# The last ConvFFN's up-products as seven half products per channel chunk instead of eight, its down-products in six groups

## The chip, the core and the metric

The kernel runs on one core of a Trainium2 chip. The metric is the device time of one execution in microseconds. TensorE (PE) does the matrix products, VectorE (DVE), ScalarE (ACT) and GpSimd (POOL) the element work, SyncE (SP) issues the weight transfers.

## What is computed

The model is one inference step of four layers on 128 context tokens and 512 latent tokens, 640 columns in all, with a model width of 1024. Each layer is a token mixer and then a gated ConvFFN, both on a normed and modulated input. The last layer's FFN is what the change touches:

```python
def _conv_ffn(h, w_up, conv_w, conv_b, w_down):
    g, u = jnp.split(h @ w_up, 2, axis=-1)       # h: tokens x 1024, w_up: 1024 x 5632
    g = _dwconv3(g, conv_w) + conv_b              # three taps along the tokens
    return (jax.nn.gelu(g, approximate=False) * u) @ w_down   # 2816 x 1024

# in _layer, for every layer:
    h = _modulate(_rmsnorm(x, P["norm2_w"][li]), sh2, sc2)
    x = x + g2[:, None, :] * _conv_ffn(h, ...)
```

## The kernel before

Activations lie with channels on the 128 partitions and tokens along the row. There are 642 columns: two that carry the modulation's shift terms, 128 of context, 512 of latents. The width 1024 is eight chunks of 128 channels (`KC`), the FFN's 2816 hidden channels are 22 chunks (`NF`), numbered f.

Every fp32 operand of a product is held as a rounded part and a remainder (names ending in h and l, XH and XL for the FFN's input). A product is three matmuls on these, h by h, h by l and l by h, for each chunk of the contraction (`mm3`). An up-product of one channel chunk is 8 chunks x 3 x 2 PSUM banks (322 and 320 columns) = 48 matmuls.

The program is a list of units, each with one weight block and a function (`unit`). The weight pipeline runs two blocks ahead (`prefetch`): SP fetches a block to `wraw` (three buffers), ACT casts it to `wh`, and DVE subtracts to get `wl` (three buffers each). Inside an engine instructions run in the order of its queue. A scheduler set that order when the kernel was built.

In the FFN, chunk f has two units, gate and up. DVE multiplies each result out of PSUM by the per-token norm `rB` (`evac`, L400). The gate then goes to `gp` on ACT (`with_bias`, L404/405), through the three taps on ACT and twice DVE (`conv3`, L420 to L422) and through Gelu on ACT (L464). DVE multiplies gate and up into `hd` (L467/468), and ACT and DVE split that into `hh` and `hl` (L410/411). After 8, 15 and 22 chunks (`THIRDS`) come eight units down, one for each output chunk d, with 8 or 7 hidden chunks as contraction. DVE adds each result to x (`x_update`, L371/372). The very last product is cut in two (`tail`), and the final norm follows.

PSUM has three two-bank buffers (`mm`) and two one-bank buffers (`smp`) in the last layers. The work pool holds three buffers of `ev`, three of `gc` and two of `hd`.

Of the kernel before, what the change touches and what calls it, by code (L numbers as in the profile page):

```python
# [77 lines left out]
def build(tc, a, plan=None):  # L78
# [96 lines left out]
    def mod(l, v, k):  # L175
        return mods[l][:, _ada_pos(v, k)]
# [17 lines left out]
    def wload(src):  # L194
        return wsplit(*wfetch(src))

    def unit(src, fn, barrier=False):
        stream["units"].append((src, fn, barrier))

    def prefetch(upto):  # L200

        us = stream["units"]
        while stream["seen"] < min(upto, stream["cap"]):
            i = stream["load"]
            if i >= len(us) or (us[i][2] and i > stream["at"]):
# [20 lines left out]
    def chunks(t, n, m=P):  # L226
        return t[:, : n * m].rearrange("p (k m) -> p k m", m=m)
# [154 lines left out]

    wk = dict(stack=None, pool=None)

    def open_work():
# [27 lines left out]

    def conv3(gp, cols, bias):

        gc = wk["pool"].tile([P, 676], F32, tag="gc", bufs=3, name="gc")[:, 0 : T + 1]
# [12 lines left out]

    def ffn(l, nxt):  # L430
        ctx = ExitStack()
        cell = dict(o={}, hid=[])

        def start():
            cell["pool"] = ctx.enter_context(tc.tile_pool(name="hid", bufs=9, reuse_waits="tile"))
# [35 lines left out]
            return fn  # L471

        def down(i, d):
            f0, f1 = THIRDS[i]

            def fn(wh, wl):
                hid = cell["hid"][f0:f1]
                hs, ls = [h for h, _ in hid], [lo for _, lo in hid]
                if nxt is None and i == 2 and d == KC - 1:
# [6 lines left out]
                x_update(d, o, mod(l, G2, d), final=(nxt,) if i == 2 else None)  # L486

            return fn


        for f in range(NF):
            unit(a["ffn_up"][l, f], up(f, 0))
            unit(a["ffn_up"][l, NF + f], up(f, 1))
            for i, (_, f1) in enumerate(THIRDS):
                if f == min(f1, NF - 1):
                    for d in range(KC):
                        unit(a[f"ffn_dn{i}"][l, d], down(i, d))
        unit(None, ctx.close)

    def tail(l, d, products):  # L500
# [831 lines left out]
    def fourier(nxt):  # L1332
# [163 lines left out]
        def place():  # L1496
            for g in range(NFG):
                for s_, d_ in zip(c["ny"], (c["fH"], c["fL"])):
                    G.dma_start(d_[2 * g + 1][0:1].bitcast(F32), s_[g : g + 1].bitcast(F32))
            fl.close()  # L1500
            open_ada(boot, 2, True)
            open_xa("left")

        def out(d):
            def fn(wh, wl):
# [294 lines left out]
```

## Time and profile before

| | before |
|---|---|
| median of 3 runs | 2715.08 us (2712.8 to 2715.26) |
| profiled execution | 2714.8 us, of which 2713.0 us are the span of the profile |
| PE busy | 2659.0 us, 98% of the span |
| DVE, ACT, POOL busy | 1803.0, 1030.0 and 119.2 us |
| the chain that ended last | PE 94%, DVE 3%, ACT 1% |

Busy shares are means over the whole program. What bounds a stage is read from a window of that stage and from what its engines waited for: behind an instruction's row in brackets stands the idle time before it and what ended it.

### The profile page before, as it was taken

Reading aid. Unit: us, or ns where it says so; the run is one execution under the profiler, and the core shown is the slowest. Engines: PE = TensorE matmul, PEld = TensorE weight load, DVE = VectorE, ACT = ScalarE, POOL = GpSimd, SP = SyncE. Lnnn points to the kernel's source line nnn. Section 1 sums busy time; section 2 is a strip of 40 time slices with the busy share of each in tenths; the row PEclk is TensorE's granted clock in tenths of the full one; section 3 lists DMA queues with packets and bytes.
Section 4 is the critical chain, followed back from the end, with each engine's and each line's share of the span. In section 5 each row is a group of like instructions: output and inputs, shape, how many; then the busy total and the mean of one; then the engine's idle time right before and its main releaser. Section 6 shows DMA issues by size and latency. Waiting matters only on the chain.

```text
span 2713.0 us, 43697 instructions
## 1 busy us (share of the span) xinstructions
PE 2659.0 (98%) x18071; PEld 2597.5 (96%) x18071; DVE 1803.0 (66%) x2855; ACT 1030.0 (38%) x1593; POOL 119.2 (4%) x153
## 2 busy tenths in 40 slices
PE   7999999999999999999999999999999999999998
PEld 6788888999999999999999999999999999999998
DVE  4677887999935689994455599954555555535354
ACT  4565675332323443232345332332332233323231
POOL 0222220000000000000001000000000000000000
PEclk9999999999999999999999999999999999999999
DMA  6223121566422325652223256622222222222221
GB/s 233 88 95 107 30 68 56 172 193 199 152 78 71 110 94 179 201 163 72 81 68 99 88 186 195 194 78 78 71 78 74 75 74 76 71 78 72 76 74 60
DMA packets 87814, 291.97 MB, mean 108 GB/s; under 512 B 11120, under 2 KB 16928, under 8 KB 87104
## 3 DMA queue, kind: packets, MB, share of 16 engines
q1 hardware_dynamic: 83808, 282.72, 33.1%
q0 software_dynamic: 2368, 4.92, 0.6%
q8 instruction: 143, 2.34, 0.4%
q10 hardware_dynamic: 1440, 1.53, 0.2%
q14 instruction: 55, 0.45, 0.1%
HBM read 283.72 MB, written 2.77 MB: 106 GB/s over the span
## 4 chain that ended last, share of the span: by engine, by line
PE 94%; DVE 3%; ACT 1%; issue 1%; DMA 1%; POOL 0%; POOLq 0%; DVEq 0%; SPq 0%; ACTq 0%
PE mm L242 80%; PE smp L763 3%; PE mm L878 1%; PE smp L900 1%; PE adaacc L166 1%; PE smp L916 1%; PE smp L915 1%; PE mm L877 1%; PE smp L809 1%; DMA adaraw<-in_ada_w 1%; PE mm L1436 1%; PE smp L337 0%; PE mm L643 0%; PE mm L1390 0%; PE mm L644 0%
## 5 line engine op out<-in xcount | busy, mean ns | idle before, releaser
L242 PE MATMUL mm<-XH,wh 128*128 128x320 f32 (+2 forms) x3248 | 750.0, 312 | 3.1 <-ACT sq L296 1.7
L242 PE MATMUL mm<-XH,wl 128*128 128x320 f32 (+2 forms) x3248 | 746.8, 311 | 0.0
L242 PE MATMUL mm<-XL,wh 128*128 128x320 f32 (+2 forms) x3248 | 745.3, 311 | 0.3 <-DVE XL L321 0.3
L190 ACT CAST wh<-wraw 128x1024 fp32r<-128x1024 f32 (+3 forms) x353 | 349.5, 991 | 961.9 <-PE mm L242 856.6
L242 PEld LDWEIGHTS mm<-XH,wh 128*128 128x128 f32 (+1 forms) x3248 | 547.3, 189 | 3.8 <-ACT sq L296 1.9
L242 PEld LDWEIGHTS mm<-XL,wh 128*128 128x128 f32 (+1 forms) x3248 | 548.1, 189 | 0.6 <-DVE XL L321 0.6
L242 PEld LDWEIGHTS mm<-XH,wl 128*128 128x128 f32 (+1 forms) x3248 | 548.0, 189 | 0.0
L191 DVE TENSOR_TENSOR wl<-wraw,wh 128x1024 fp32r<-128x1024 f32 (+3 forms) x333 | 394.7, 1185 | 28.7 <-ACT wh L190 27.6
L158 DVE CUSTOM_DVE_ANT_0 adajunk<-adaraw,adarow,sm 128x1024 f32<-128x1024 f32 x304 | 389.0, 1280 | 4.6 <-DMA adaraw<-in_ada_w 1.6
L400 DVE TENSOR_TENSOR ev<-mm,rB 128x642 f32<-128x642 f32 x200 | 164.9, 825 | 305.5 <-PE mm L242 299.9
L242 PE MATMUL mm<-hh,wh 128*128 128x320 f32 (+1 forms) x1536 | 350.5, 309 | 0.0
L242 PE MATMUL mm<-hh,wl 128*128 128x320 f32 (+1 forms) x1536 | 350.4, 309 | 0.0
L242 PE MATMUL mm<-hl,wh 128*128 128x320 f32 (+1 forms) x1536 | 350.1, 309 | 0.0
L242 PEld LDWEIGHTS mm<-hl,wh 128*128 128x128 f32 x1536 | 256.8, 188 | 0.0
L242 PEld LDWEIGHTS mm<-hh,wh 128*128 128x128 f32 x1536 | 256.8, 188 | 0.0
L242 PEld LDWEIGHTS mm<-hh,wl 128*128 128x128 f32 x1536 | 256.6, 188 | 0.0
L371 DVE SCALAR_TENSOR_TENSOR x<-mm,mod,x 128x128 f32<-128x128 f32 x111 | 38.9, 350 | 293.5 <-PE mm L242 293.4
L410 ACT CAST hh<-hd 128x640 fp32r<-128x640 f32 x96 | 69.9, 728 | 208.6 <-DVE hd L468 190.8
L464 ACT ACTIVATE gc<-gc 128x641 f32<-128x641 f32 x88 | 65.4, 743 | 176.4 <-DVE gc L422 176.3
L421 DVE SCALAR_TENSOR_TENSOR gc<-gp,conv,gc 128x641 f32<-128x641 f32 x88 | 77.9, 886 | 53.8 <-ACT gc L420 53.8
L411 DVE TENSOR_TENSOR hl<-hd,hh 128x640 fp32r<-128x640 f32 x96 | 79.0, 823 | 45.7 <-ACT hh L410 45.7
L420 ACT ACTIVATE gc<-gp,conv 128x641 f32<-128x641 f32 x88 | 81.5, 926 | 2.9
(333 smaller groups left out, 2994.4 us busy)
## 6 DMA issues: line engine op xcount, KB each, us to landing
adaraw<-in_ada_w SPq DMA_DIRECT2D x192, 512.0 KB, 3.8
wraw<-in_ffn_up SPq DMA_DIRECT2D x176, 512.0 KB, 3.6
wraw<-in_ffn_dn SPq DMA_DIRECT2D x64, 448.0 KB, 3.2
wraw<-in_ffn_dn SPq DMA_DIRECT2D x32, 512.0 KB, 3.7
wraw<-in_sconv_win SPq DMA_DIRECT2D x24, 512.0 KB, 3.6
wraw<-in_wo SPq DMA_DIRECT2D x8, 512.0 KB, 3.6
wraw<-in_fnet_w SPq DMA_DIRECT2D x8, 512.0 KB, 3.6
wraw<-in_sconv_wout SPq DMA_DIRECT2D x8, 512.0 KB, 3.5
```

The lines of the kernel that those rows point to most:

```text
L158: V.tensor_tensor_reduce(junk, w, ada["row"][:, r], 1.0, vec("adab", l * 48 + h * 8 + k), ALU.mult, ALU.add, m)
L190: S.copy(h[:, :n], raw[:, :n])
L191: (eng or V).tensor_tensor(lo[:, :n], raw[:, :n], h[:, :n].bitcast(F32), ALU.subtract)
L242: TE.matmul(o[:m, c0:c1], w_[:, k], x_[k][:, x0 : x0 + c1 - c0], start=st, stop=sp)
L371: V.scalar_tensor_tensor(x[:, d, 0:TP], o[:, lo : lo + TP], g[:, 0:1], x[:, d, 0:TP], ALU.mult, ALU.add)
L400: V.tensor_tensor(t[:m], o[:m, 190:832], st["rB"][:m], ALU.mult)
L410: S.copy(h, v)
L411: V.tensor_tensor(lo, v, h.bitcast(F32), ALU.subtract)
L420: S.activation(gc, gp[:, 1:642], AF.Identity, bias=bias, scale=cols[:, 1:2])
L421: V.scalar_tensor_tensor(gc, gp[:, 0:641], cols[:, 0:1], gc, ALU.mult, ALU.add)
L464: S.activation(gc, gc, AF.Gelu)
L763: TE.matmul(o[:, 0 : c1 - c0], w_[:, k], x_[k][:, c0:c1], start=st_, stop=sp)
```

## The change

In the last layer (`seven`), chunks 0 to 2 stay as they are. For f = 3 to 21 the two 1024 x 128 weight blocks (gate and up) and the 642 columns of the input are cut into halves. That makes a 2 x 2 by 2 x 2 block product: two halves of the contraction (four chunks each), gate and up, left 322 and right 322 columns (they overlap by two). Instead of eight products of half size the kernel does seven, on sums and differences of the blocks (Winograd's form of Strassen's scheme):

- `operands(k)`, four times: POOL adds XH and XL back together for two chunks (128 x 642), DVE forms four differences of 322 columns, ACT casts them, and DVE splits them. k = 0, 1 stand behind chunk 1 and k = 2, 3 behind chunk 2.
- `weights(f, j)`, j = 0 to 3: both blocks of f are fetched at j = 0. POOL makes three combinations at j = 0 and one at j = 2, each 128 x 512. ACT and DVE cast and split seven half blocks.
- `up7(f, j)`: seven `product`s of 12 matmuls of 322 columns, each in a one-bank `smp` buffer. ACT copies the first result to `m1`, DVE adds the others out of PSUM into `tg` and `tu` (seven additions) and then multiplies both by `rB`. `gated` and `later` put the bias, conv, Gelu and `hd` of chunk f between the products of chunk f+1. For chunk 21 they follow at once.
- The down-products come in six groups (`SMALL`), after chunks 4, 8, 12, 15, 18 and 21, of 4, 4, 4, 3, 3 and 4 hidden chunks: 48 units of half the length instead of 24.
- Ahead of the last layer's mixer `drop` opens the pools anew: two buffers of `ev` and `gc` instead of three, PSUM with two `mm` and four `smp` buffers instead of three and two.

```diff
...
+SMALL = ((0, 4, 0, 0), (4, 8, 0, 4), (8, 12, 1, 0), (12, 15, 1, 4), (15, 18, 2, 0), (18, 22, 2, 3))
+HW = 322
+NORMAL = 3
+SUMS = ((), (0, 1), (2, 3))
...
+        LEFT, RIGHT = slice(0, HW), slice(W - HW, W)
+
+        def operands(k):
...
+                for d in (k, k + 4):
+                    t = wk["pool"].tile([P, W], F32, tag="ev", bufs=wk["bufs"], name="ev")
+                    G.tensor_tensor(t, st["xh"][d].bitcast(F32), st["xl"][d].bitcast(F32), ALU.add)
+                    b.append(t)
+                (b11, b12), (b21, b22) = [(t[:, LEFT], t[:, RIGHT]) for t in b]
+                u = [wk["pool"].tile([P, 676], F32, tag="hd", name="hd") for _ in range(2)]
+                t1, t2, t3, t4 = [u[i // 2][:, i % 2 * HW : i % 2 * HW + HW] for i in range(4)]
+                V.tensor_tensor(t1, b12, b11, ALU.subtract)
+                V.tensor_tensor(t2, b22, t1, ALU.subtract)
+                V.tensor_tensor(t3, b22, b12, ALU.subtract)
+                V.tensor_tensor(t4, b21, t2, ALU.subtract)
+                for t, (h, lo) in zip((t1, t2, t3, t4), cell["t"]):
+                    S.copy(h[:, k], t)
+                    V.tensor_tensor(lo[:, k], t, h[:, k].bitcast(F32), ALU.subtract)
...
+        def weights(f, j):
...
+                def part(i, v):
+                    c_ = slice(i * 512, i * 512 + 512)
+                    S.copy(h[:, c_], v)
+                    V.tensor_tensor(lo[:, c_], v, h[:, c_].bitcast(F32), ALU.subtract)
+
+                if j == 0:
+                    s3 = cell["s3"] = cell["pool"].tile([P, 512], F32, tag="s3", bufs=1, name="s3")
+                    part(0, a11)
+                    G.tensor_tensor(s3, a11, a21, ALU.subtract)
+                    G.tensor_tensor(a21, a21, a22, ALU.add)
+                    G.tensor_tensor(a11, a21, a11, ALU.subtract)
+                    part(1, a11)
+                elif j == 1:
+                    part(0, cell["s3"])
+                    part(1, a22)
+                elif j == 2:
+                    part(0, a21)
+                    part(1, a12)
+                    G.tensor_tensor(a12, a12, a11, ALU.subtract)
+                else:
+                    part(0, a12)
...
+        def product(o, i, wh, wl, xh, xl):
...
+            for k in range(4):
+                for w_, x_, e in ((h, xh, False), (h, xl, False), (lo, xh, k == 3)):
+                    TE.matmul(o[:, 0:HW], w_[:, k], x_[k], start=k == 0 and x_ is xh and w_ is h, stop=e)
...
+                if j == 0:
+                    product(o, 0, wh, wl, *half(0, LEFT))
+                    product(q, 1, wh, wl, *sums(1))
+                    S.copy(m1, o[:, 0:HW])
+                    V.tensor_tensor(tg[:, RIGHT], m1, q[:, 0:HW], ALU.add)
+                    later()
+                elif j == 1:
+                    product(o, 0, wh, wl, *sums(2))
+                    product(q, 1, wh, wl, *sums(3))
+                    V.tensor_tensor(tu[:, RIGHT], tg[:, RIGHT], o[:, 0:HW], ALU.add)
+                    V.tensor_tensor(tu[:, 0:n], tu[:, n : 2 * n], q[:, 0:n], ALU.add)
+                    later()
+                elif j == 2:
+                    product(o, 0, wh, wl, *sums(0))
+                    product(q, 1, wh, wl, *half(4, LEFT))
+                    V.tensor_tensor(tu[:, RIGHT], tu[:, RIGHT], o[:, 0:HW], ALU.add)
+                    V.tensor_tensor(tg[:, RIGHT], tg[:, RIGHT], o[:, 0:HW], ALU.add)
+                    V.tensor_tensor(tu, tu, rB, ALU.mult)
+                    V.tensor_tensor(tg[:, 0:n], m1[:, 0:n], q[:, 0:n], ALU.add)
+                else:
+                    product(o, 0, wh, wl, *half(4, RIGHT))
+                    V.tensor_tensor(tg[:, RIGHT], tg[:, RIGHT], o[:, 0:HW], ALU.add)
+                    V.tensor_tensor(tg, tg, rB, ALU.mult)
+                    gated(f, tg, tu)
+                    if f == NF - 1:
+                        later()
+                        later()
...
```

How this moves the queues is seen at three places. The first is DVE's queue over one chunk in the middle of the last FFN. Before, one chunk's rows are these (`ev` from PSUM, a whole block's `wl`, the two taps, then `hd` and `hl`):

```order
L400 TENSOR_TENSOR ev<-mm,rB 128x642
L191 TENSOR_TENSOR wl<-wraw,wh 128x1024
L421 SCALAR_TENSOR_TENSOR gc<-gp,conv,gc 128x641
L422 SCALAR_TENSOR_TENSOR gc<-gp,conv,gc 128x641
L400 TENSOR_TENSOR ev<-mm,rB 128x642
L191 TENSOR_TENSOR wl<-wraw,wh 128x1024
L467 SCALAR_TENSOR_TENSOR hd<-ev,gc 128x128
L468 SCALAR_TENSOR_TENSOR hd<-ev,gc 128x512
L411 TENSOR_TENSOR hl<-hd,hh 128x640
```

With the change a chunk has 21 rows in that queue. These are twelve of them, from the first addition of a chunk (`smp` is a one-bank result in PSUM, the `ev` on both sides are `tg` and `tu`) to the additions of its third step:

```order
L595 TENSOR_TENSOR ev<-m_23697,smp 128x322
L427 SCALAR_TENSOR_TENSOR gc<-gp,conv,gc 128x641
L541 TENSOR_TENSOR wl<-wraw,wh 128x512
L428 SCALAR_TENSOR_TENSOR gc<-gp,conv,gc 128x641
L541 TENSOR_TENSOR wl<-wraw,wh 128x512
L634 SCALAR_TENSOR_TENSOR hd<-ev,gc 128x128
L635 SCALAR_TENSOR_TENSOR hd<-ev,gc 128x512
L600 TENSOR_TENSOR ev<-ev,smp 128x322
L541 TENSOR_TENSOR wl<-wraw,wh 128x512
L601 TENSOR_TENSOR ev<-ev,smp 128x320
L417 TENSOR_TENSOR hl<-hd,hh 128x640
L606 TENSOR_TENSOR ev<-ev,smp 128x322
```

The taps and `hd` of the chunk before now stand ahead of L600, which frees a PSUM buffer of this chunk.

The second place is POOL's queue where the seven-product chunks begin. Before, nothing stands there between the norms of the last layer. Now it holds the weight combinations of chunks 3 and 4 (L546 to L556) mixed with the operand sums (L513):

```order
L546 TENSOR_TENSOR s_22678<-wraw 128x512
L547 TENSOR_TENSOR wraw<-wraw 128x512
L513 TENSOR_TENSOR ev<-XH,XL 128x642
L548 TENSOR_TENSOR wraw<-wraw 128x512
L513 TENSOR_TENSOR ev<-XH,XL 128x642 x4
L556 TENSOR_TENSOR wraw<-wraw 128x512
L513 TENSOR_TENSOR ev<-XH,XL 128x642
L546 TENSOR_TENSOR s_22920<-wraw 128x512
L547 TENSOR_TENSOR wraw<-wraw 128x512
L513 TENSOR_TENSOR ev<-XH,XL 128x642 x2
L548 TENSOR_TENSOR wraw<-wraw 128x512
L556 TENSOR_TENSOR wraw<-wraw 128x512
```

From there on each chunk brings POOL the four rows L546, L547, L548 and L556.

The third place is DVE's queue at the same point, behind chunk 2's product: its gate's last tap and its `hd`, and then the operands of k = 2 (all its rows) and the first row of k = 3:

```order
L428 SCALAR_TENSOR_TENSOR gc<-gp,conv,gc 128x641
L541 TENSOR_TENSOR wl<-wraw,wh 128x512 x2
L479 SCALAR_TENSOR_TENSOR hd<-ev,gc 128x128
L480 SCALAR_TENSOR_TENSOR hd<-ev,gc 128x512
L518 TENSOR_TENSOR hd<-ev 128x322
L519 TENSOR_TENSOR hd<-ev,hd 128x322
L417 TENSOR_TENSOR hl<-hd,hh 128x640
L524 TENSOR_TENSOR tm<-hd,tm 128x322
L520 TENSOR_TENSOR hd<-ev 128x322
L521 TENSOR_TENSOR hd<-ev,hd 128x322
L524 TENSOR_TENSOR tm<-hd,tm 128x322 x3
L518 TENSOR_TENSOR hd<-ev 128x322
```

Before, the evacuation of chunk 3's gate followed `hl` there at once. Now the rows of the operands of k = 2 and k = 3 lie between.

## Rows read from the trace of the kernel before

**Rows 1.** The page: span, busy time by engine, and the chain that ended last.

```profile
span 2713.0 us, 43697 instructions
PE 2659.0 (98%) x18071; PEld 2597.5 (96%) x18071; DVE 1803.0 (66%) x2855; ACT 1030.0 (38%) x1593; POOL 119.2 (4%) x153
...
PE 94%; DVE 3%; ACT 1%; issue 1%; DMA 1%; POOL 0%; POOLq 0%; DVEq 0%; SPq 0%; ACTq 0%
```

**Rows 2.** Windows: seven channel chunks up, then seven units down, last FFN.

```profile
2256.40:2356.20 99.80, 99.80 (x675) 99.80 (x674) 52.84 (x63) 38.62 (x50) 0.00 (x0) 1.00 0.26 79
2363.40:2412.70 49.30, 49.30 (x338) 49.30 (x337) 14.99 (x22) 7.38 (x8) 0.00 (x0) 1.00 0.23 75
```

**Rows 3.** DVE in time over one channel chunk: start, duration, engine, instruction.

```profile
2277.97 0.83 DVE L400 TENSOR_TENSOR ev<-mm,rB 128x642 f32<-128x642 f32 x1 [2.57 <-PE mm L242]
...
2280.84 0.89 DVE L421 SCALAR_TENSOR_TENSOR gc<-gp,conv,gc 128x641 f32<-128x641 f32 x1 [0.86 <-ACT gc L420]
2281.77 0.89 DVE L422 SCALAR_TENSOR_TENSOR gc<-gp,conv,gc 128x641 f32<-128x641 f32 x1
...
2287.03 0.35 DVE L467 SCALAR_TENSOR_TENSOR hd<-ev,gc 128x128 f32<-128x128 f32 x1
2287.29 0.74 DVE L468 SCALAR_TENSOR_TENSOR hd<-ev,gc 128x512 f32<-128x512 f32 x1
2288.83 0.83 DVE L411 TENSOR_TENSOR hl<-hd,hh 128x640 fp32r<-128x640 f32 x1 [0.79 <-ACT hh L410]
2292.22 0.83 DVE L400 TENSOR_TENSOR ev<-mm,rB 128x642 f32<-128x642 f32 x1 [2.57 <-PE mm L242]
```

**Rows 4.** ACT in time over the same chunk.

```profile
2278.83 0.41 ACT L404 ACTIVATE gp<-ev 128x128 f32<-128x128 f32 x1
...
2279.89 0.92 ACT L420 ACTIVATE gc<-gp,conv 128x641 f32<-128x641 f32 x1
2282.69 0.74 ACT L464 ACTIVATE gc<-gc 128x641 f32<-128x641 f32 x1 [1.88 <-DVE gc L422]
...
2288.07 0.73 ACT L410 CAST hh<-hd 128x640 fp32r<-128x640 f32 x1 [2.22 <-DVE hd L468]
```

**Rows 5.** DVE in time, two units down.

```profile
2370.44 0.35 DVE L371 SCALAR_TENSOR_TENSOR x<-mm,mod,x 128x128 f32<-128x128 f32 x1 [4.90 <-PE mm L242]
...
2377.49 0.35 DVE L371 SCALAR_TENSOR_TENSOR x<-mm,mod,x 128x128 f32<-128x128 f32 x1 [4.90 <-PE mm L242]
```

**Rows 6.** PE in time, layer 0: a product that fills one PSUM bank.

```profile
379.95 0.31 PE L763 MATMUL smp<-qH,wl 128*128 128x320 f32 x1
...
380.83 0.31 PE L763 MATMUL smp<-qH,wl 128*128 128x320 f32 x1
```

**Rows 7.** Instructions by shape, whole span: count, busy us, mean ns, idle before.

```profile
L191 DVE TENSOR_TENSOR wl<-wraw,wh 128x512 fp32r<-128x512 f32 x1 | 0.7, 680 | 0.0
L619 DVE TENSOR_TENSOR ev<-smp,rB 128x322 f32<-128x322 f32 x1 | 0.5, 491 | 0.0
L191 POOL TENSOR_TENSOR wl<-wraw,wh 128x512 fp32r<-128x512 f32 x3 | 3.9, 1286 | 1.0 <-ACT wh L190 0.9
L781 POOL TENSOR_TENSOR qs<-qs,sin 128x320 f32<-128x320 f32 x4 | 3.5, 872 | 1.2 <-DVE qs L779 1.2
```

**Rows 8.** POOL and DVE in time, layer 0: wl beside POOL, and alone.

```profile
373.87 0.91 POOL L891 TENSOR_SCALAR pt<-pt,sums 128x768 f32<-128x768 f32 x1 [1.14 <-DVE sums L890]
...
373.98 1.86 DVE L191 TENSOR_TENSOR wl<-wraw,wh 128x1024 fp32r<-128x1024 f32 x1 [0.28 <-ACT wh L190]
...
382.79 1.23 DVE L191 TENSOR_TENSOR wl<-wraw,wh 128x1024 fp32r<-128x1024 f32 x1 [0.53 <-POOL pt L891]
```

**Rows 9.** The same engines: ol beside POOL, and ol alone.

```profile
147.70 0.91 POOL L891 TENSOR_SCALAR pt<-pt,sums 128x768 f32<-128x768 f32 x1 [0.72 <-DVE sums L890]
...
148.06 1.23 DVE L588 TENSOR_TENSOR ol<-os,oh 128x640 fp32r<-128x640 f32 x1 [0.45 <-ACT oh L587]
...
353.04 0.83 DVE L588 TENSOR_TENSOR ol<-os,oh 128x640 fp32r<-128x640 f32 x1 [0.20 <-ACT oh L587]
```

More of the change, by code (lines that the diff above doesn't have):

```diff
@@ L391, in open_work @@
         wk["i"] = 0
+        wk["bufs"] = bufs
     def close_work():
@@ L431, in ffn @@
         ctx = ExitStack()
-        cell = dict(o={}, hid=[])
+        cell = dict(o={}, hid=[], late=[])
+        seven = l == DEPTH - 1
+        groups = SMALL if seven else tuple((f0, f1, i, 0) for i, (f0, f1) in enumerate(THIRDS))
         def start():
-            cell["pool"] = ctx.enter_context(tc.tile_pool(name="hid", bufs=9, reuse_waits="tile"))
+            cell["pool"] = ctx.enter_context(tc.tile_pool(name="hid", bufs=5 if seven else 9, reuse_waits="tile"))
+            if seven:
+                cell["t"] = [
+                    [cell["pool"].tile([P, 4, HW], F32R, tag=f"t{i}{j}", bufs=1, name="tm") for j in "hl"] for i in range(4)
+                ]
             cell["conv"] = cell["pool"].tile([P, NF, 4], F32, tag="conv", bufs=1, name="conv")
@@ L473, in down @@
         def down(i, d):
-            f0, f1 = THIRDS[i]
+            f0, f1 = groups[i][:2]
+            last = i == len(groups) - 1
             def fn(wh, wl):
@@ L478, in fn @@
                 hs, ls = [h for h, _ in hid], [lo for _, lo in hid]
-                if nxt is None and i == 2 and d == KC - 1:
+                if nxt is None and last and d == KC - 1:
                     tail(l, d, lambda o, part: mm3(o, wh, wl, hs, ls, f1 - f0, False, apart=CUT, part=part))
@@ new lines, in gated, with one, two @@
+        def gated(f, gt, ut):
+            c_ = {}
+            def one():
+                gp = next_gp()
+                with_bias(gp, 1, 130, gt)
+                cols = cell["conv"][:, f]
+                c_["g"] = conv3(gp, cols, cols[:, 3:4])
+            def two():
+                gc = c_["g"]
+                S.activation(gc, gc, AF.Gelu)
+                hd = wk["pool"].tile([P, 676], F32, tag="hd", name="hd")[:, 0:T]
+                V.scalar_tensor_tensor(hd[:, 0:TP], ut[:, 2:130], ut[:, 0:1], gc[:, 0:128], ALU.add, ALU.mult)
+                V.scalar_tensor_tensor(hd[:, TP:T], ut[:, 130:642], ut[:, 1:2], gc[:, 129:641], ALU.add, ALU.mult)
+                cell["hid"].append(split_hid(cell["pool"], hd))
+            cell["late"] += [one, two]
@@ L495, in ffn @@
+        for f in range(NF):
+            if seven and f >= NORMAL:
+                for j in range(4):
+                    unit(weights(f, j), up7(f, j))
+            else:
+                unit(a["ffn_up"][l, f], up(f, 0))
+                unit(a["ffn_up"][l, NF + f], up(f, 1))
+                if seven:
+                    for k in SUMS[f]:
+                        unit(None, operands(k))
+            for i, (_, f1, t, c0) in enumerate(groups):
                 if f == min(f1, NF - 1):
                     for d in range(KC):
-                        unit(a[f"ffn_dn{i}"][l, d], down(i, d))
+                        w = a[f"ffn_dn{t}"][l, d]
+                        if seven:
+                            w = w[:, c0 * P : (c0 + groups[i][1] - groups[i][0]) * P]
+                        unit(w, down(i, d))
@@ L1611, in build, with drop @@
         if s_ == "mix":
+            if l == DEPTH - 1:
+                def drop():
+                    close_work()
+                    boot.close()
+                    open_work(2)
+                    open_psum(2, 4)
+                unit(None, drop)
             mixers[l](nxt)
```

46 lines of the change are left out of this document (37 added, 9 removed).

## The prediction

> **What bounds the kernel now.** I read the page first: PE is busy 2659.0 of 2713.0 us, and the chain that ended last is 94% PE [rows 1]. The profiled run took 2714.8 us, 1.8 more than its span and 0.3 less than the median of the three runs, 2715.08, so I make the sum against 2714.8. Then I read windows inside the last FFN. In both of them, up and down, PE is busy in every microsecond at a granted clock of 1.00. DVE is busy 52.84 of 99.80 us, ACT 38.62 and POOL not at all [rows 2]. So only PE's matmuls set the time there, and DVE has nearly half of it to spare. The rows of DVE in time show how the spare time is used. DVE waits for PE before each evacuation (2.57 and 2.44 us), and an evacuation never comes late [rows 3]. A kernel with fewer matmuls gains their time as long as DVE, ACT and POOL can still follow. That has to be worked out for each place.
>
> **The gain on PE.** One chunk up takes 2292.22 - 2277.97 = 14.25 us [rows 3] for 96 matmuls, half of 322 and half of 320 columns, 148.5 ns each. One unit down of 48 matmuls of 320 columns takes 2377.49 - 2370.44 = 7.05 us [rows 5], 146.9 ns each. By difference one of 322 columns takes about 150. A chunk is now 84 of them, 12.6 us. The new products fill one PSUM bank at a time where the old ones alternate between two. Layer 0 shows this form at the same pace: six starts in 380.83 - 379.95 = 0.88 us, 147 ns [rows 6]. So 19 chunks gain 19 x (14.25 - 12.6) = **-31**. At 146.9 ns for each matmul it would be -36, at 150.4 ns -31, the bounds. The units down keep their number of matmuls (half as long, twice as many): 0 on PE.
>
> **DVE's load per chunk.** Before, 7.5 us per 14.25 (52.84 for seven) [rows 2]. Now each chunk has seven splits of 512 columns, seven additions, two multiplications by rB, two taps, hd and hl. Their rows: 0.680 for a split, 0.491 for an addition of 322 columns with one input in PSUM [rows 7], 0.83 for the multiplication of 642 columns by the evacuation's row, 0.89 for a tap, 0.35 + 0.74 for hd, 0.83 for hl [rows 3]. In a full queue instructions start some 0.06 us before the last one ends (2287.29 after 2287.03 + 0.35, [rows 3]), two taps lie 0.93 apart. So 7 x 0.62 + 7 x 0.43 + 2 x 0.78 + 2 x 0.92 + 0.92 + 0.78 = 12.45 us, against 12.6 for PE. DVE also waits inside a chunk. Behind L613 the queue holds a split and L595, 1.05 us, and then a tap that needs the bias and the first tap on ACT: 2279.89 + 0.92 - 2278.83 = 1.98 [rows 4]. The splits that follow need casts queued behind these two ACT steps. Gelu takes 0.74 [rows 4] before hd. I put the waits at 2.2 us together, an estimate from these rows, and get D = 14.7 us per chunk without any disturbance. So DVE, not PE, sets the pace of the up-chunks.
>
> **POOL beside DVE.** Each chunk brings POOL four operations of 128 x 512, 1.286 us each [rows 7], 5.1 us. What they do to DVE can be seen in layer 0. The same split of 1024 columns took 1.23 us alone, and 1.86 when a POOL operation of 0.91 us had begun 0.11 us earlier [rows 8]. Another (ol) took 0.83 alone and 1.23 beside POOL [rows 9]. In both cases the DVE instruction ended about as if it had begun when POOL ended (373.87 + 0.91 + 1.23 = 376.01, seen 375.84; 147.70 + 0.91 + 0.83 = 149.44, seen 149.29). So DVE with two inputs in SBUF waits while POOL reads SBUF. Splits, taps, rB, hd and hl are of that kind, 9.4 of the 12.45 us. The additions read PSUM, and layer 0 has no row of such a one beside POOL to price. The bounds are no loss at all (POOL falls into the additions' 3.0 us and the 2.2 us of waits) and the whole 5.1 us. I take the middle, 2.6, because POOL waits for the data of the same queue and so sometimes falls in DVE's own waits: **D = 17.3**, bounds 14.7 and 19.8.
>
> The Trainium skill, page "SBUF — State Buffer", section "Who interferes with whom", says that a DVE instruction with two SBUF inputs contends with a GpSimd instruction that reads SBUF, and that whoever issues first holds the shared ports for the whole instruction while the other fully blocks. The two rows agree with it. By that rule taken at its word the loss would lie near the whole 5.1 us, and the sum would be that of the third rival below, 2765, where my middle value gives 2732.
>
> **What D costs.** PE cannot start the last product of a chunk until L600 has freed its buffer (four one-bank buffers, seven products). At the first chunk of a stretch (the chunks between two groups of units down) the gate of the chunk before has run beside the units down, and L600 comes right behind the third product: 36 x 0.15 + 0.43 = 5.9 us after the stretch begins. PE needs it at 72 x 0.15 = 10.8: a reserve of 4.9 us. Each further chunk uses up D - 12.6. A stretch of n chunks loses (n - 1)(D - 12.6) - 4.9, and the units down that follow let DVE catch up: one old unit held 14.99 / 7 = 2.14 us of DVE in 7.05 [rows 2], one new half unit about 1.6 in 3.5. There are two stretches of four (5 to 8, 9 to 12), three of three, and one of two (3 and 4). With D = 17.3: 2 x 9.2 + 3 x 4.5 + nothing for the short one, which starts late after the operands, about 1 to 2 for it: **+33**. With D = 14.7: +3. With 19.8: 2 x 16.7 + 3 x 9.5 + 2.3 = +64. The extra x_updates cost nothing while PE covers them as above.
>
> **The start.** After chunk 2's last product, PE has the first product and the k = 0, 1 parts of four others ready: 36 matmuls, 5.4 us. The operands of k = 2 need an `ev` buffer, and there are two, both held by chunk 2, the second until its hd. POOL's sum of 642 columns has no row: 0.872 for 320 and 1.286 for 512 [rows 7] give 1.57, against 1.7 by twice the 320. From the end of the product: gate out 0.8 (behind the operands of k = 0 and 1), ACT 1.98, taps with the other evacuation between them 2.6, Gelu 0.74, hd 0.92, one POOL sum 1.57, four differences 4 x 0.43, all from the rows named: 10.4. PE waits 5.0. Then k = 3: two sums, 3.1, and a first difference, cast and split, about 1.2, so 14.7, while PE's 12 matmuls of k = 2 end at 12.2: 2.5 more, and about 2 for the last splits one by one. **+10**, with 9 and 11.5 as bounds (POOL's two sums beside DVE's splits).
>
> **The end.** Chunk 21 has no later chunk to hide its gate. From the end of its last product: L612 and L613 1.2, ACT 1.98, taps 1.84, Gelu 0.74, hd 0.92, hh 0.73 [rows 4], hl 0.78: 8.2 us. PE has the first three hidden chunks of two units, 36 matmuls of 147 ns, 5.3. The wait is 2.9, or 6 if DVE's queue is some 3 us late as it is at D = 17.3. **+5**. At the other five groups chunk f's gate also comes last in the group, but its products follow after other matmuls of the stretch's first units; hidden unless DVE is late, and then part of D's price.
>
> **Other edits.** `drop` takes a third `ev`, `gc` and `mm` away in the mixer and chunks 0 to 2: an evacuation begins within 0.1 us of its product's end, and the next product covers 7.1 us of it [rows 3]. Zero. The weights come in the same bytes; POOL's edits of `wraw` hold two of three buffers longer, hidden with two blocks ahead.
>
> **Sum.** 2714.8 - 31 + 33 + 10 + 5 = 2731.8: **2732 us**, 0.6% slower.
>
> **Rivals.**
> 1. DVE keeps up, and the kernel is faster. POOL falls into additions and waits, D at most about 15.4. With 14.7: 2714.8 - 31 + 3 + 9 + 3 = 2699, and with a gain of 36 or an even shorter D 2696 at the lowest, 2709 at the highest. For it: DVE's dense work is below PE's 12.6 us. Against it: the rows of layer 0. It decides at D = 15.9: then the stretches lose 2 x 5.0 + 3 x 1.7 + 1 = 16, and start, end and stretches take back the 31. Chance 0.27.
> 2. The chunk takes D of 15.5 to 16.3: the loss is 11 to 20, and the time is 2710 to 2720, no change that a measurement can tell (0.2% is 5.4 us, about what one can tell here). Chance 0.13.
> 3. Each POOL operation holds DVE up in full, D = 19.8: 2714.8 - 31 + 64 + 11.5 + 6 = 2765. For it: the two rows of layer 0, where the whole overlap was lost. Against it: a quarter of DVE's work reads PSUM. Chance 0.12, from about 2752.
> 4. My forecast's case, D from 16.3 to 18.6, 2720 to 2752: chance 0.48.
>
> Range 2700 to 2756: a part of rival 1 lies below it and most of rival 3 above it, together under 2 in 10. The forecast's own range is 2720 to 2752. Faster 0.27, same 0.13, slower 0.60.
>
> **What would show it.** Right: PE's starts of chunks 6 to 8 lie some 17 us apart and those of the first chunk of a stretch 12.6; PE waits for DVE L600 and for `tm`; DVE is busy nearly all of an up-stretch, and its splits of 512 columns vary from 0.68 to above 1.5 us where a POOL row overlaps. Wrong: chunks every 12.6 to 13 us with DVE waiting for PE (D was overrated), or splits that keep 0.68 beside POOL. A matmul pace other than 150 ns would change the gain itself, and a granted clock below 1.00 after the waits at the start would add to all of it.

## The result, and the profile after

The changed kernel takes 2736.08 us, median of four runs (2735.37 to 2738.04). The kernel before took 2715.17 us beside it (four runs, 2712.8 to 2715.82). The ratio is 1.0079, with a 95% interval of 1.0067 to 1.0092: 21 us slower. The forecast was 2732, 17 slower. The sum came out right, but several of its terms did not, as the rows below show.

The page of the changed kernel answers to [rows 1]: span, busy time, and the chain that ended last.

```profile
span 2733.8 us, 44148 instructions
PE 2642.0 (97%) x17843; PEld 2571.9 (94%) x17843; DVE 1961.1 (72%) x3187; ACT 1082.7 (40%) x1747; POOL 239.2 (9%) x239
...
PE 85%; DVE 9%; ACT 3%; issue 1%; DMA 1%; POOL 1%; POOLq 0%; DVEq 0%; SPq 0%; ACTq 0%
```

PE works 17.0 us less than before (2659.0 to 2642.0), and its idle time grows from 54.0 to 91.8 us, by 37.8. The span grows by the difference, 20.8. The chain that ended last shows where the time goes: PE falls from 94% to 85%, DVE rises from 3% to 9%.

The waits of PE over the whole span (line waited in, who was waited for: total us, times, longest):

```profile
PE smp L569 <- DVE ev L600: 20.0, 9, 4.1
...
PE mm L247 <- ACT hh L416: 4.6, 1, 4.6
...
PE smp L569 <- ACT tm L523: 4.3, 2, 2.2
...
PE smp L569 <- DVE tm L524: 2.7, 3, 1.1
...
PE smp L569 <- ACT m L594: 2.1, 1, 2.1
...
PE smp L569 <- DVE wl L541: 1.4, 1, 1.4
```

These six are 35.1 of the 37.8 us. The waits for L600 lie in the stretches of chunks (between two groups of units down), the four rows with `tm`, `m` and `wl` at the start, in chunk 3, and `hh` at the end.

PE saved 17 us of work where the matmul count gives 31. The windows say why (PE, PEld, DVE, ACT and POOL busy, then the granted clock as the first number behind POOL's count):

```profile
2225.00:2278.00 53.00, 51.19 (x350) 50.92 (x349) 34.21 (x46) 21.95 (x37) 13.48 (x9) 1.00 0.13 41
2278.60:2300.00 21.40, 12.92 (x42) 9.82 (x42) 19.10 (x28) 6.12 (x12) 9.83 (x7) 0.53 0.13 36
2300.00:2331.00 31.00, 31.00 (x211) 30.85 (x210) 26.32 (x46) 14.74 (x24) 1.86 (x2) 1.00 0.24 77
2384.00:2387.50 3.50, 3.50 (x15) 3.50 (x16) 3.50 (x8) 1.57 (x4) 0.00 (x0) 0.54 0.00 0
```

Up to 2278 the clock is 1.00. That is the end of PE's first wait at the start, 2.1 us. Its other waits there follow, and until 2300 it is granted 0.53, the lower of its two levels (1.2 GHz) nearly all the time. It is 1.00 again after some 5 us of work without a wait. A wait of 4.1 us at the third chunk of a stretch brings the same for 3.5 us. The matmuls of 322 columns show it directly (PE in time, on both sides of the return to 1.00):

```profile
2297.28 0.47 PE L569 MATMUL smp<-tm,wh 128*128 128x322 f32 x1
2297.54 0.47 PE L569 MATMUL smp<-tm,wl 128*128 128x322 f32 x1
...
2300.09 0.31 PE L569 MATMUL smp<-XH,wh 128*128 128x322 f32 x1
2300.23 0.31 PE L569 MATMUL smp<-XL,wh 128*128 128x322 f32 x1
```

Their starts lie 0.26 to 0.27 apart and then 0.14 to 0.15. Most of the 14 us between 31 and 17 are this clock: 35 matmuls at the start, some 14 behind each of three waits in the stretches and 11 at the end come 0.12 us later each, about 11 us together. The rest is mostly the last matmul before each wait, whose full 0.31 us (0.47 at the low clock) counts as busy, as no next one begins inside it.

Inside a stretch DVE now sets the pace. L613 ends a chunk on DVE:

```profile
2357.48 0.82 DVE L613 TENSOR_TENSOR ev<-ev,rB 128x642 f32<-128x642 f32 x1
...
2389.53 0.82 DVE L613 TENSOR_TENSOR ev<-ev,rB 128x642 f32<-128x642 f32 x1
...
2403.58 0.82 DVE L613 TENSOR_TENSOR ev<-ev,rB 128x642 f32<-128x642 f32 x1
```

The first two stand 32.05 us apart with one L613 between them (at 2373.40), so 16.0 us per chunk, against 14.25 in [rows 3] and 12.6 that PE needs. The last comes 14.05 later; beside that chunk POOL has only one operation, since units down follow.

DVE in time in the second (first row) and third chunk of this stretch, and then POOL in the same two chunks:

```profile
2366.55 1.78 DVE L417 TENSOR_TENSOR hl<-hd,hh 128x640 fp32r<-128x640 f32 x1
...
2373.40 0.81 DVE L613 TENSOR_TENSOR ev<-ev,rB 128x642 f32<-128x642 f32 x1
...
2376.26 0.89 DVE L427 SCALAR_TENSOR_TENSOR gc<-gp,conv,gc 128x641 f32<-128x641 f32 x1 [0.47 <-ACT gc L426]
2377.06 0.68 DVE L541 TENSOR_TENSOR wl<-wraw,wh 128x512 fp32r<-128x512 f32 x1
2377.67 1.91 DVE L428 SCALAR_TENSOR_TENSOR gc<-gp,conv,gc 128x641 f32<-128x641 f32 x1
2379.50 1.75 DVE L541 TENSOR_TENSOR wl<-wraw,wh 128x512 fp32r<-128x512 f32 x1
...
2381.44 1.77 DVE L635 SCALAR_TENSOR_TENSOR hd<-ev,gc 128x512 f32<-128x512 f32 x1
2383.24 0.49 DVE L600 TENSOR_TENSOR ev<-ev,smp 128x322 f32<-128x322 f32 x1
```

```profile
2366.37 1.28 POOL L548 TENSOR_TENSOR wraw<-wraw 128x512 f32<-128x512 f32 x1 [1.56 <-DVE wl L541]
...
2377.04 1.86 POOL L546 TENSOR_TENSOR s<-wraw 128x512 f32<-128x512 f32 x1 [0.79 <-DMA wraw<-in_ffn_up]
2378.97 1.73 POOL L547 TENSOR_TENSOR wraw<-wraw 128x512 f32<-128x512 f32 x1
2381.40 1.26 POOL L548 TENSOR_TENSOR wraw<-wraw 128x512 f32<-128x512 f32 x1 [0.69 <-DVE wl L541]
```

The tap L428 takes 1.91 us where L422 took 0.89 [rows 3]. The split takes 1.75 for 0.68 [rows 7], the second part of hd 1.77 for 0.74, and hl 1.78 for 0.83. Each began while a POOL row was running, and ended 0.55 to 0.7 us after POOL's row did: L546 ends at 2378.90 and L428 at 2379.58, L547 at 2380.70 and the split at 2381.25. POOL waits too: L546 takes 1.86 instead of 1.29, beside the split of 2377.06, whose recorded start is 0.02 us behind its own. The Trainium skill, page "SBUF — State Buffer", section "Who interferes with whom", says that a DVE instruction with two SBUF inputs contends with a GpSimd instruction that reads SBUF, and that the order of issue decides which of them waits. These rows agree, but two starts 0.02 us apart do not show which came first. L600 behind the four rows is late, and PE waits for it:

```profile
2366.77 0.39 PE L569 MATMUL smp<-XH,wh 128*128 128x322 f32 x1 [0.74 <-DVE ev L600]
...
2383.88 0.39 PE L569 MATMUL smp<-XH,wh 128*128 128x322 f32 x1 [4.10 <-DVE ev L600]
```

The start, DVE in time behind chunk 2's product, which ended at about 2271.6:

```profile
2274.05 0.81 DVE L406 TENSOR_TENSOR ev<-mm,rB 128x642 f32<-128x642 f32 x1
...
2281.20 1.76 DVE L480 SCALAR_TENSOR_TENSOR hd<-ev,gc 128x512 f32<-128x512 f32 x1
...
2284.81 1.53 DVE L519 TENSOR_TENSOR hd<-ev,hd 128x322 f32<-128x322 f32 x1 [1.45 <-POOL ev L513]
2286.27 1.89 DVE L417 TENSOR_TENSOR hl<-hd,hh 128x640 fp32r<-128x640 f32 x1
...
2289.29 4.00 DVE L524 TENSOR_TENSOR tm<-hd,tm 128x322 fp32r<-128x322 f32 x3
```

Chunk 2's gate leaves PSUM at 2274.05, 2.5 us after that end, because the operands of k = 1 stand ahead of it. (The gate's half of the product had ended some 7.1 us before, at about 2264.4.) My chain let it begin at the end itself. Then four groups of rows are longer than alone: hd by 1.0, a difference by 1.05, hl by 1.05, and three tm splits take 4.00 for 1.29.

### The profile page after: what moved, and what is told of

It reads as the page before. It is cut to its first block, busy times and chain, and to the rows that moved or that the text cites. A ratio compares the mean times of both kernels' runs of the same rounds, so it can differ in the third digit from the quotient of the medians.

```text
span 2733.8 us, 44148 instructions
## 1 busy us (share of the span) xinstructions
PE 2642.0 (97%) x17843; PEld 2571.9 (94%) x17843; DVE 1961.1 (72%) x3187; ACT 1082.7 (40%) x1747; POOL 239.2 (9%) x239
## 4 chain that ended last, share of the span: by engine, by line
PE 85%; DVE 9%; ACT 3%; issue 1%; DMA 1%; POOL 1%; POOLq 0%; DVEq 0%; SPq 0%; ACTq 0%
PE mm L247 68%; PE smp L569 3%; PE smp L923 3%; DVE wl L541 1%; PE mm L1038 1%; PE smp L1060 1%; PE adaacc L171 1%; PE smp L1076 1%; PE smp L1075 1%; PE mm L1037 1%; PE smp L969 1%; DMA adaraw<-in_ada_w 1%; DVE gc L428 1%; PE mm L1596 1%; DMA wraw<-in_ffn_up 0%
## 5 line engine op out<-in xcount | busy, mean ns | idle before, releaser
L195 ACT CAST wh<-wraw 128x1024 fp32r<-128x1024 f32 (+4 forms) x339 | 314.3, 928 | 819.9 <-PE mm L247 703.3
L247 PE MATMUL mm<-XH,wh 128*128 128x322 f32 (+1 forms) x2640 | 610.7, 312 | 3.5 <-DVE x L1166 2.6
L247 PE MATMUL mm<-XH,wl 128*128 128x322 f32 (+1 forms) x2640 | 607.2, 311 | 0.0
L247 PE MATMUL mm<-XL,wh 128*128 128x322 f32 (+1 forms) x2640 | 605.6, 311 | 0.3 <-DVE XL L326 0.3
L247 PEld LDWEIGHTS mm<-XH,wl 128*128 128x128 f32 (+1 forms) x2640 | 445.2, 189 | 0.0
L247 PE MATMUL mm<-hh,wh 128*128 128x320 f32 x1536 | 351.4, 309 | 4.6 <-ACT hh L416 4.6
L247 PE MATMUL mm<-hl,wh 128*128 128x320 f32 x1536 | 350.9, 309 | 0.0
L247 PE MATMUL mm<-hh,wl 128*128 128x320 f32 x1536 | 350.4, 309 | 0.0
L569 PE MATMUL smp<-tm,wh 128*128 128x322 f32 x608 | 140.6, 318 | 9.1 <-ACT tm L523 4.3
L569 PEld LDWEIGHTS smp<-tm,wh 128*128 128x128 f32 x608 | 104.7, 193 | 12.1 <-ACT tm L523 5.8
```

Of the source, the lines that this page charges most:

```text
L195: S.copy(h[:, :n], raw[:, :n])
L247: TE.matmul(o[:m, c0:c1], w_[:, k], x_[k][:, x0 : x0 + c1 - c0], start=st, stop=sp)
L569: TE.matmul(o[:, 0:HW], w_[:, k], x_[k], start=k == 0 and x_ is xh and w_ is h, stop=e)
```

## The experiments

Each run is compared with runs of the kernel before on the same chip, whose medians were 2713.9 to 2715.6 us. The changed kernel itself stands at 2736.1. Differences from it are across chips.

**Without POOL's operations on the weights.**

```diff
-                    G.tensor_tensor(s3, a11, a21, ALU.subtract)
-                    G.tensor_tensor(a21, a21, a22, ALU.add)
-                    G.tensor_tensor(a11, a21, a11, ALU.subtract)
...
-                    part(0, cell["s3"])
+                    part(0, a21)
...
-                    G.tensor_tensor(a12, a12, a11, ALU.subtract)
```

> The four POOL operations on the weight blocks of each seven-product chunk are left out; the raw half blocks are cast and split in their place, so the output is not the reference's and every other instruction stays. In the changed kernel the seven-product chunks inside a stretch came 16.0 us apart and DVE's rows there were some 1.2 us per chunk longer than alone. Theory (POOL's reads delay DVE, DVE sets the pace): the pace falls to about 14.8 us, the splits of 512 columns all take 0.68, and 13 follow-on chunks gain 1.2 each, so about 2720 us. Rival (the pace comes from the chain of gate, taps and Gelu through two ev buffers, POOL beside it is harmless): pace 16 as before, 2733 to 2737.

Measured 2702.15 us, ratio to before 0.9949 (0.9934 to 0.9963): 34 us less than the changed kernel, twice what my theory gave. The window of a whole stretch of four chunks:

```profile
2338.10:2388.10 50.00, 50.00 (x337) 49.79 (x336) 42.74 (x75) 26.22 (x45) 0.00 (x0) 1.00 0.24 74
```

PE is busy in every microsecond at a clock of 1.00. The stretch takes 50.1 us from its first matmul to that of the next group, 12.5 per chunk. The 26 us that the stretches lost are all gone, and so are the start's waits in part (7.2 us instead of 10.5; chunks 3 and 4 take 38.6 us instead of 43.2). The rival is out.

**POOL writes, but reads nothing.**

```diff
-                    G.tensor_tensor(s3, a11, a21, ALU.subtract)
-                    G.tensor_tensor(a21, a21, a22, ALU.add)
-                    G.tensor_tensor(a11, a21, a11, ALU.subtract)
+                    for t in (s3, a21, a11):
+                        G.memset(t, 0.5)
+                        G.memset(t, 0.25)
...
-                    G.tensor_tensor(a12, a12, a11, ALU.subtract)
+                    G.memset(a12, 0.5)
+                    G.memset(a12, 0.25)
```

> Each of the four POOL operations per chunk is replaced by two constant fills of the same half block, so POOL writes SBUF but reads nothing, in about the same place and for about 1 us; the output is not the reference's. Theory (it is POOL's reading that holds DVE up): as without POOL, about 2720 us, with splits at 0.68 us beside POOL rows. Rival 1 (any POOL access, writes too, holds DVE up): 2733 to 2737, longer splits beside POOL rows. Rival 2 (not the ports but waiting for POOL's results costs time): the results still have to be waited for, so 2730 or more although the splits take 0.68.

Measured 2703.35 us, 0.9953 (0.9936 to 0.997), as without POOL. DVE's groups by shape in the stretches (count, busy, mean ns):

```profile
L541 DVE TENSOR_TENSOR wl<-wraw,wh 128x512 fp32r<-128x512 f32 x102 | 69.5, 685 | 5.9 <-ACT wh L540 5.6
L428 DVE SCALAR_TENSOR_TENSOR gc<-gp,conv,gc 128x641 f32<-128x641 f32 x17 | 15.0, 883 | 0.1
```

Both are at their plain durations, 0.68 and 0.88. In the changed kernel the same groups had means of 0.739 and 1.335. The two fills that stand for an operation take 0.53 us each, so POOL writes for 4.2 us per chunk, where the four operations took 5.1 or more. So it is POOL's reading of SBUF that costs the time, not its writing, and not the wait for its results.

**Operands one chunk earlier.**

```diff
-SUMS = ((), (0, 1), (2, 3))
+SUMS = ((0, 1), (2, 3), ())
```

> The operands of k = 0 and 1 stand behind chunk 0 and those of k = 2 and 3 behind chunk 1, one chunk earlier. Theory (the wait at the start is the operands' chain being late, and the low clock there follows from the wait): PE's 10.5 us of waits in chunk 3 go and its clock stays at 1.00, chunk 3 and 4 take some 26 to 28 us instead of 43, about 2719 us. Rival 1 (the queue work only moves: DVE then delays the evacuations of chunks 1 and 2, with two mm buffers left): at most 5 us gained, 2731 or more. Rival 2 (the clock falls for another reason): the waits go but the low clock stays, about 2725.

Measured 2734.52 us, 1.0064 (1.0049 to 1.0079), 1.5 us less than the changed kernel. The first rival holds. PE's waits, and DVE's splits of k = 0 with the evacuation behind the operands of k = 1:

```profile
PE smp L569 <- DVE ev L600: 22.3, 10, 4.1
...
PE mm L247 <- DVE ev L406: 3.4, 1, 3.4
```

```profile
2250.89 5.17 DVE L524 TENSOR_TENSOR tm<-hd,tm 128x322 fp32r<-128x322 f32 x3
...
2260.32 0.81 DVE L406 TENSOR_TENSOR ev<-mm,rB 128x642 f32<-128x642 f32 x1
```

The three splits took 5.17 us beside two POOL sums and a weight operation, and PE waited 3.4 us for an evacuation behind them. Chunks 3 and 4 take 35 us instead of 43, but begin 5.2 us later, and the stretches after them lose 1.4 more.

**Chunk 21 by eight products.**

```diff
-NORMAL = 3
+SEVEN = range(3, 21)
...
                 if which == 0:
+                    later()
+                    later()
                     return
...
-            if seven and f >= NORMAL:
+            if seven and f in SEVEN:
```

> Chunk 21 is done by eight products again, so its gate starts at half its time; chunk 20's late steps then follow chunk 21's gate product. Theory (the end costs a 4.6 us wait for hh and about 2 us of low clock, because the gate chain begins at the end of the last product): these 6.5 us go, 1.6 us of matmuls come back, and the last stretch is one follow-on chunk shorter, 3 less: about 2728 us. Rival (DVE's backlog is what is late at the end, whatever the last chunk's form): a wait of 3 us or more stays and the gain is lost, 2734 to 2738.

Measured 2726.53 us, 1.004 (1.0025 to 1.0055), 9.6 less. The wait for `hh` is gone. The end's price and its place are as in the theory.

**Only the groups and the buffers.**

```diff
-NORMAL = 3
-SUMS = ((), (0, 1), (2, 3))
+NORMAL = NF
+SUMS = ((), (), ())
```

> All 22 chunks keep eight products; only the six groups down and the smaller buffer counts of the last layer remain of the change. Theory (the 24 extra units, x_updates and the lost buffers are covered by PE): no difference to the kernel before, within 2 us of 2714.8. Rival (half units of 3.5 us leave DVE or the evacuations with two mm buffers late at the groups' starts): 2718 or more with waits for DVE's x_update or ev.

Measured 2716.1 us, 1.0007 (0.9998 to 1.0017): 1.5 us over the kernel before, which cannot be told from zero, as my sum had it.

**The weight combinations on DVE.** All four `G.tensor_tensor` of `weights` become `V.tensor_tensor`:

```diff
-                    G.tensor_tensor(s3, a11, a21, ALU.subtract)
+                    V.tensor_tensor(s3, a11, a21, ALU.subtract)
...
-                    G.tensor_tensor(a12, a12, a11, ALU.subtract)
+                    V.tensor_tensor(a12, a12, a11, ALU.subtract)
```

> The four combinations of each chunk's weight blocks are made by DVE in place of POOL, the rest stays and the output is the reference's. Without POOL's reads the chunks came 14.05 and 13.49 apart on DVE, with them 16.0. Theory (what counts is DVE's time, and POOL's reading costs it 2.2 us per chunk): four operations of 0.62 in the queue add 2.5, the pace is about 16.2, no row is lengthened, the time 2733 to 2742. Rival (POOL's slowness or the hand-over between the engines is the price, not DVE's time): the pace falls below 15 and the time to 2722 or less.

Measured 2708.86 us, 0.9981 (0.9972 to 0.9991). My expectation failed: the kernel is 27 us faster than with POOL, and faster than before the change. DVE in time over one chunk of the middle of a stretch, then the window of two chunks:

```profile
2352.74 0.82 DVE L613 TENSOR_TENSOR ev<-ev,rB 128x642 f32<-128x642 f32 x1
...
2357.01 0.88 DVE L428 SCALAR_TENSOR_TENSOR gc<-gp,conv,gc 128x641 f32<-128x641 f32 x1
2357.81 0.68 DVE L546 TENSOR_TENSOR s<-wraw 128x512 f32<-128x512 f32 x1
2358.52 0.69 DVE L547 TENSOR_TENSOR wraw<-wraw 128x512 f32<-128x512 f32 x1
...
2367.66 0.82 DVE L613 TENSOR_TENSOR ev<-ev,rB 128x642 f32<-128x642 f32 x1
```

```profile
2353.50:2383.60 30.10, 28.50 (x191) 27.99 (x190) 29.07 (x52) 15.33 (x27) 0.00 (x0) 1.00 0.19 62
```

The pace is 14.92 us, all rows have their plain length, and DVE is busy 29.07 of 30.10 us. I had added 2.5 us to the 13.49 and 14.05 of the run with writes only. There, however, DVE waited for PE, and those paces were not its own limit. The right base is the 12.45 us of the prediction's sum of DVE's rows: 12.45 + 4 x 0.62 = 14.93.

**One operand set per chunk.**

```diff
-NORMAL = 3
-SUMS = ((), (0, 1), (2, 3))
+NORMAL = 4
+SUMS = ((0,), (1,), (2,), (3,))
```

> The four operand sets stand behind chunks 0, 1, 2 and 3, one each, and chunk 3 is done by eight products. Theory (the start is lost because two sets, 7 us of DVE and 6 us of POOL with the gate's rows between, do not fit behind one chunk): with one set per chunk the waits of the start fall from 10.5 us to under 4 and the low clock with them, 1.6 us of matmuls come back, about 2722 us. Rival (the last set's chain of gate, hd, POOL sum and differences is what is late, whatever lies before it): a wait of 5 us and more and a low clock stay in chunk 4, 2728 or more.

Measured 2727.46 us, 1.0049 (1.0034 to 1.0064), 8.6 less than the changed kernel. That lies between the two, at the rival's edge. PE's waits in the last layer's FFN, the end's `hh` left out:

```profile
PE smp L569 <- DVE ev L600: 18.0, 9, 4.1
PE smp L569 <- ACT tm L523: 5.6, 1, 5.6
```

The start's 10.5 us in seven waits have become one of 5.6. A set right behind the last normal chunk is late even alone.

**No two seven-product chunks in a row.**

```diff
-NORMAL = 3
-SUMS = ((), (0, 1), (2, 3))
+SEVEN = (4, 5, 7, 9, 11, 13, 15, 16, 18, 19)
+SUMS = ((0,), (1,), (2,), (3,))
```

(with the `later` calls and the `SEVEN` test as for chunk 21 above)

> Ten chunks only are done by seven products (4, 5, 7, 9, 11, 13, 15, 16, 18, 19), so that no two follow each other inside a stretch, with one operand set behind each of chunks 0 to 3. Theory (a single seven-product chunk fits into DVE's reserve, because the chunk after it brings DVE 7.5 us in 14.25): the waits for L600 and at the end go, the gain is 10 x 1.6 = 16, less about 3 at the start: about 2702 us, under both kernels. Rival (the seven-product form costs by itself, its gate or its first products being late even when alone): 2712 or more.

Measured 2709.36 us, 0.9983 (0.9973 to 0.9992), between theory and rival. PE's longest waits from chunk 0 to the last group (L597 of this kernel is the addition that is L595 in the changed one):

```profile
PE smp L571 <- ACT tm L525: 5.5, 1, 5.5
PE smp L571 <- DVE ev L597: 2.2, 4, 0.9
```

The waits for L600's addition are gone, and so is the low clock in the stretches. 2.2 us in four short waits for a chunk's first addition are new. What is missing is the start's wait, 5.5 us, with its low clock. The last operand set stood right ahead of chunk 4.

**Half of POOL's operations.**

```diff
-                    G.tensor_tensor(a11, a21, a11, ALU.subtract)
...
-                    G.tensor_tensor(a12, a12, a11, ALU.subtract)
```

> Two of the four POOL operations of each chunk (L548 and L556) are left out, so the output is not the reference's; the other two, which begin as soon as the weights have landed, stay. With all four the follow-on chunks came 16.0 us apart, without any reading 12.6. Theory (each POOL operation that reads SBUF takes 0.9 us from DVE): pace 14.2, the stretches lose 5 to 9 us instead of 26, about 2713 to 2719 us. Rival (the two that wait for DVE and hand the last weights back late are the price): as without POOL, 2702 to 2706.

Measured 2713.81 us, 0.9995 (0.9986 to 1.0005), inside the theory's range and far from the rival's. Its parts were off: the follow-on chunks with POOL beside them come 14.7 to 16.0 us apart, not 14.2, and the stretches lose 10 us, not 5 to 9. The waits for L600's addition fall from 20.0 to 6.9 us. DVE in time:

```profile
2373.43 1.99 DVE L428 SCALAR_TENSOR_TENSOR gc<-gp,conv,gc 128x641 f32<-128x641 f32 x1
...
2379.61 0.82 DVE L417 TENSOR_TENSOR hl<-hd,hh 128x640 fp32r<-128x640 f32 x1
```

The tap beside L546 and L547 (POOL from 2373.45 to 2376.57) is still twice its length. hl, which lay beside L548, has its plain 0.82 again.

**Combinations on DVE, operands spread with a chunk between, and chunk 21 by eight products.** The edits of three runs above together, with `SEVEN = range(5, 21)` and `SUMS = ((0,), (1,), (2,), (3,), ())`.

> Chunks 5 to 20 by seven products, with the weight combinations on DVE, one operand set behind each of chunks 0 to 3, chunk 4 between, chunk 21 by eight products. Theory (start, stretches and end are separate prices): 16 x 1.6 = 26 gained, 3 to 5 lost in the stretches at a pace of 15.0 us, nothing at the start and the end: 2690 to 2696 us. Rival (the operands cost the same wherever they stand, because chunks 0 to 4 then evacuate late): a wait of 4 us or more with low clock stays, 2698 or more.

Measured 2692.24 us, 0.9917 (0.9902 to 0.9932): 23 us under the kernel before, the fastest version found. PE's longest wait from chunk 1 to the last group (L602 is the addition that is L600 in the changed kernel):

```profile
PE smp L571 <- DVE ev L602: 3.0, 2, 1.5
```

Only 3.0 us are left of the start's, the stretches' and the end's waits. The sum of gains and losses by separate prices holds.

**The same with the operands sooner**, `SEVEN = range(4, 21)` and `SUMS = ((0, 1), (2,), (3,), ())`.

> As the one before, but chunks 4 to 20 by seven products and the operands behind chunks 0 (two sets), 1 and 2. Theory: one more chunk gained, 1.6 us, if the two sets behind chunk 0 stay inside the spare time of chunks 0 to 2: 2688 to 2695 us. Rival (two sets behind one chunk delay the evacuation of the next, as when they stood behind chunk 1): a wait of 3 us for an evacuation and a low clock, 2695 to 2700.

Measured 2696.38 us, 0.9931 (0.9916 to 0.9946), as the rival has it, though the wait for an evacuation is only 1.2 us. Another 2.6 us are waits in chunk 4. One more seven-product chunk does not pay for the two sets behind chunk 0.

**Only the operand sums on DVE.**

```diff
-                    G.tensor_tensor(t, st["xh"][d].bitcast(F32), st["xl"][d].bitcast(F32), ALU.add)
+                    V.tensor_tensor(t, st["xh"][d].bitcast(F32), st["xl"][d].bitcast(F32), ALU.add)
```

> Only the eight sums of 128 x 642 for the operands go from POOL to DVE; the weight combinations stay on POOL. In the changed kernel chunks 3 and 4 took 43 us of PE's time in place of 25. Theory (the start is mostly POOL's reading: behind chunk 2 the rows of hd, one difference, hl and three tm splits are 5.9 us longer than alone, and chunk 2's gate came out of PSUM 2.5 us late): the rows keep their lengths, DVE's eight sums of 0.8 us take less than POOL's of 1.6, chunks 3 and 4 come down to 34 to 37 us, 2727 to 2731 us. Rival (the chain of gate, Gelu, hd and the two ev buffers is what takes the time at the start): less than 3 us gained, 2733 or more.

Measured 2731.43 us, 1.0063 (1.0046 to 1.008), 4.7 less than the changed kernel. Chunks 3 and 4 take 38.9 us instead of 43.2. So some 4 of the start's 18 us were POOL's sums, less than I expected. hd and one difference behind chunk 2 are still 1.0 to 1.1 us longer, beside weight operations, and without those the two chunks took 38.6 (the first run). POOL's two kinds of work are thus some 4 to 5 us of the start each; both were not taken away at once. A wait of 6.1 us for the first `tm` of k = 2 stays, though the gate leaves PSUM 2.8 us sooner. I take the chain of gate, Gelu and hd behind it for the rest of the start, as the rival has it, but no run isolates it.

## Why the prediction was right, and where its terms were not

**The gain, -31: right.** Undisturbed chunks take 12.5 us (the run without POOL's operations) where 12.6 was forecast, and the difference to 14.25 for 19 chunks gives 31 to 33. The matmul pace in one bank is 0.147 to 0.15, as in [rows 6].

**The pace D: 17.3 forecast, 16.0 measured.** The mechanism was right: DVE's queue sets the pace, and POOL's reading slows it. The split into parts was wrong. I put 2.2 us for waits inside a chunk on top of 12.45 of work. The run with the combinations on DVE shows that a full queue has hardly any waits: its 14.92 us hold 14.6 of busy time, and 12.45 + 2.5 = 14.93, so the 12.45 already cover its waits. In the two chunks timed above DVE is busy 14.16 and 15.14 us. Rows made longer by POOL are 2.1 and 3.1 of that, which leaves 12.0 of work in both, and DVE waits 1.8 and 1.0. So the 2.6 for longer rows was about right, and the terms too large were the waits and, a little, the work. Against the 12.45 of a full queue without POOL, an estimate, its operations cost 16.0 - 12.45 = 3.5 of their 5.1 us: some waits of DVE for what POOL and ACT hand on later come on top of the longer rows.

**What D costs, +33.** The stretches of chunks 5 to 21 lost 26 us by PE's rows (6.7, 6.9, 2.9, 5.1 and 4.6 us over 12.6 per chunk), low clock included. By my formula D = 16.0 would give 16 to 17. Two steps failed in it. One is the reserve of 4.9 us: 20.0 us are waits. I took L600 as it lies in a stretch's first chunk. From the second on, the taps and hd of the chunk before stand ahead of L600, so that its second start (2366.15) lies 17.9 us behind its first (2348.24), not 16.0, and PE already waits there, 0.74 us at 2366.77 and again 4.1 in the chunk after. The other is the clock, which I had left at 1.00: some 5 us of the 26 are matmuls at the low one. A pace taken too high cancelled against both.

**The start, +10 forecast, 18 measured** (chunks 3 and 4 take 43.2 us, of which 25.5 are the matmuls of 150 ns). The chain was named right, but its first step was put at the product's end. The gate came out 2.5 us late, and POOL's operations made rows 5.9 us longer (the four groups above) where I had allowed 1.5 us at most. I had also counted 36 matmuls as ready. PE came to 30, because the fifth product needs one of the four one-bank buffers, and the first of them was freed by ACT's copy L594 only at 2278.2: the wait of 2.1 us. About 4 us of the 18 are the low clock (35 matmuls at 0.27 in place of 0.15).

**The end, +5: right in place and nearly in size.** The wait is 4.6 us, 1 to 2 us of low clock follow, and the run without it gains 9.6, of which the sum of the theory explains 8.

**The zeros** (extra units, x_updates, fewer buffers) came to 1.5 us in the run with these alone, inside its noise.

**The term that was missing** is the clock. The prediction named it among what could make it wrong, but gave it no value. It cost about 11 us, most of the 14 us of PE's time that were not saved. The three waits were put at 48 us together. The measured waits are 35.1, and with those 14 they are 49. That the total was met within 4 us is therefore in part luck, two errors that cancel: waits that were too long, at a clock that was too fast.

**The rivals.** DVE keeping up (the first) is what happens without POOL's reads: 2702 to 2703 us in the two runs that show it. POOL holding DVE up in full (the third) does not hold on average, since 3.5 of 5.1 us are lost. Single rows lose about 1.0 of a POOL row's 1.29 us.

## What to carry to other kernels

Before work is given to an idle engine, look at what the busy one reads at that time. Here GpSimd's four operations of 1.29 us cost VectorE about 3.5 us per chunk, and the same four cost only 2.5 us on VectorE itself. Where a change takes matmuls away, add up the other engines' queues first, as a full queue (here 12.45 us beside 12.6) leaves nothing for a disturbance. And where PE will wait for several us, see whether the clock stays at 1.00 behind the wait, and give the matmuls there a price at the lower level too.

## What the runs showed of the hardware that was not expected

- PE's granted clock fell to 0.5 behind three of the nine waits for L600, those of 3.4 to 4.1 us, behind the end's wait of 4.6, and behind the start's first of 2.1. Behind the other six waits for L600, of 0.7 to 2.9 us, it stayed at 1.00. With half of POOL's operations it fell behind two of 2.5 and 2.6 us: here the length of a wait alone does not tell. At 0.5 matmuls of 322 columns came 0.27 us apart in place of 0.15, for 3.5 us after one wait of 4.1, and for over 20 us through the start's chain of short waits. Over the last FFN that was about 11 us, beside the 20 us waited for L600.
- Constant fills by GpSimd of the same half blocks, 0.53 us each, left VectorE's splits at 0.685 us and the tap at 0.883. Reading operations brought single ones to 1.75 and 1.9 us.
- Three small tm splits in a row took 5.17 us beside three GpSimd operations that followed each other, against 1.29 alone.
